# RWKV-7 elementwise tiles made in the projections instead of the scan, and projection weights split once per stream

## The chip, the cores and the metric

One Trainium2 chip, one core of it. The metric is the device time of one execution of the whole program in microseconds (us). The core has five engines that run side by side: TensorE (PE, matrix products; PEld are its weight loads), VectorE (DVE), ScalarE (ACT), GpSimd (POOL) and SyncE (SP), which here mainly issues DMA transfers. Each engine takes its instructions in the order in which the program holds them, and a waiting instruction holds up what stands behind it on its engine.

## The reference

A trunk of two layers (width 1024, 16 heads of 64 channels) for 1024 prompt tokens and for 8 short sequences of 8 sample tokens. Layer 0 mixes by a convolution, layer 1 by RWKV-7; each layer also has attention to a memory and an MLP of hidden width 4096. The change touches the RWKV-7 mixer alone:

```python
r = xr @ w_r;  k = xk @ w_k;  v = xv @ w_v            # projections of shifted, mixed inputs
decay = exp(-exp(w_log))                              # w_log from w0 + tanh(xw @ w1) @ w2
a = sigmoid(a0 + (xa @ a1) @ a2);  g = sigmoid(xg @ g1) @ g2
kk = k * k_k;  kk = kk / max(sqrt(sum(kk * kk)), L2_EPS)    # per head
k = k * (1 + (a - 1) * k_a)
y, s = wkv7_scan(r, decay, k, v, -kk, kk * a, s0)           # s: 64x64 per head, step by step
y = standardize(y) * lnx_g + lnx_b
bonus = sum(r * k * r_k) * v                                # per head
out = ((y + bonus) * g) @ w_o
```

## The kernel before

Channels lie on the 128 partitions in 8 blocks (a block is a *pair* of heads, index `m`), tokens run along the free axis. All wide products take float32 operands that are split into a high and a low half: `split` (L95) casts the high half on ScalarE (L96) and subtracts it for the low half on VectorE (L97), and `prod` (L138) does three matmuls (L142 to L144) for each product. Weights come from memory as tiles `raw` and become `wt` with both halves.

**Two streams.** Stream A is part 0 (512 prompt tokens, in column tiles of 256), stream B part 1 (the other 512 prompt tokens and the 64 sample tokens, in column tiles of 288). Each stream is a generator that runs conv, attention, MLP of layer 0, then the RWKV projections (`projections`, L729), the RWKV scan in chunks of 64 tokens (`scan`, L1088: A chunks 0 to 7, B the samples and chunks 8 to 15), the output projection (`mixer_out`, L893), attention and MLP of layer 1. B's scan needs A's last state. `pace` (L916) interleaves the two: each `yield` gives a cost, and the stream with the lower sum of costs goes next. A timeline scheduler then sets the order of each engine, which is fixed before the program runs. A_d and B_d are the PSUM accumulators of the two streams.

**Projections.** `project` (L866) does one of the three wide products, r, k and v in turn, block by block, and stores each result block (L847, issued by ScalarE) in the memory tile `scr[part][m]`, which has six rows: v, r, k, decay, a, g. Beside it run generators handed in as `sides`: `hidden` (L797) makes the hidden layers of the low-rank products, `lora` (L849) their outputs. The hidden layers of w and a share the tile `one`; so `lora("a")` runs last, when all else of the projections is done. A keeps the low halves of its 24 weight tiles: `load` (L106) with `share` puts them in the memory tiles `low` (`put`, L99), and B loads them from there rather than subtracting again.

**Scan.** `prep` (L1153) loads one chunk (`ld` four rows, `v` one row; eight DMAs each, one per pair, L1151, on SyncE's queue) and makes of it, in tiles of 128x512: kk, its square, the cumulative sum of the log decay (a VectorE scan), two exponentials, the products a, r, b and k with them (`ar`, `bk`), the sums of squares (`ss`, four matmuls on `sq`), and the bonus (`bon`, a product with `bones`, the matrix of ones per head). `invert`, `solve` and `step` are the recurrence itself. Its banks are p_pp, p_pz and p_half. `finish` (L1452) normalizes, applies lnx_g, lnx_b, bonus and gate on GpSimd, and stores `yg`. `prep` of one chunk, `inverse` of the chunk before and `rest` of the one before that run interleaved (`run`, L1514).

## Time and profile before

| | |
|---|---|
| time, median of 3 runs | 3836.46 us (3828.97 to 3836.49) |
| time of the profiled execution | 3837.42 us |
| span of the profiled execution | 3835.7 us |
| TensorE busy | 3623.9 us (94%) |
| VectorE busy | 2351.6 us (61%) |
| ScalarE busy | 1610.0 us (42%) |
| GpSimd busy | 660.7 us (17%) |
| mean granted clock of TensorE | 0.955 |
| moved by DMA | 456.03 MB, mean 119 GB/s |

The span is what the trace covers; the program's time is 1.7 us more. Busy TensorE time contains time at a reduced clock, so a busy share of 94% is not 94% of its peak. In the page's pictures a span is cut into 40 slices of 96 us.

The stretches that matter here, in us from the start: A's projections beside B's first MLP 1335 to 1747; A's scan 1747 to 2130 (beside it the end of B's MLP, B's norm and the start of B's projections); B's projections, A's memory layer, A's output projection and the start of its attention 2130 to 2460; B's scan to about 2850, beside A's attention and second MLP; then B's output projection, attention and MLP, with A's MLP until about 3395.

### The profile page before, as it was taken

The page shows a single profiled execution, that of the slowest core. Times are in us where ns is not written, and L with a number is a line of the kernel's source. Part 1 is how long each engine was busy: PE and PEld are TensorE (multiplying, and loading weights), DVE is VectorE, ACT ScalarE, POOL GpSimd, SP SyncE. Part 2 cuts the span into 40 slices and gives each one's busy share as a digit, 9 for nine tenths or more (in the row PEclk, how much of TensorE's full clock was granted, in tenths as well). Part 3 has the DMA queues.
Part 4 walks back from the last instruction along what each step waited for, and adds up shares of the span by engine and source line. Part 5 has one row for each costly group of instructions (what it writes and reads, how often), then busy time and mean ns, then how long its engine had stood idle before and what let it go on. Part 6 is the DMA issues. An engine that isn't in the chain of part 4 may idle for free.

```text
span 3835.7 us, 75763 instructions
## 1 busy us (share of the span) xinstructions
PE 3623.9 (94%) x30906; PEld 3369.6 (88%) x30906; DVE 2351.6 (61%) x4479; ACT 1610.0 (42%) x3190; POOL 660.7 (17%) x704
## 2 busy tenths in 40 slices
PE   8989979999999999999979998879999999989998
...
PEclk9999989999999999999979998889899999989998
...
GB/s 226 132 53 129 80 67 106 102 114 170 153 90 83 126 151 152 159 138 112 85 88 109 232 254 146 111 93 70 54 113 120 114 120 197 121 72 83 83 83 64
DMA packets 333004, 456.03 MB, mean 119 GB/s; under 512 B 155248, under 2 KB 247664, under 8 KB 332656
## 3 DMA queue, kind: packets, MB, share of 16 engines
...
q14 instruction: 105, 0.86, 0.1%
...
## 4 chain that ended last, share of the span: by engine, by line
PE 77%; DVE 11%; ACT 4%; DMA 4%; issue 2%; POOL 1%; SPq 1%; ACTq 0%; DVEq 0%; POOLq 0%
PE B_d L142 11%; PE B_d L144 11%; PE B_d L143 11%; PE A_d L142 10%; PE A_d L143 9%; PE A_d L144 9%; PE A_d L362 3%; PE B_d L362 2%; DMA scr<-t_st 1%; SPq L1151 1%; PE A_hd L810 1%; PE A_d L442 1%; PE B_sa L608 1%; DVE wt L97 1%; PE B_sa L610 1%
## 5 line engine op out<-in xcount | busy, mean ns | idle before, releaser
L97 DVE TENSOR_TENSOR wt<-raw,wt 128x1024 fp32r<-128x1024 f32 x447 | 567.3, 1272 | 476.9 <-ACT wt L96 473.0
L96 ACT CAST wt<-raw 128x1024 fp32r<-128x1024 f32 x488 | 508.5, 1047 | 502.2 <-PE B_d L144 268.6
L142 PE MATMUL B_d<-hAB,wt 128*128 128x288 f32 (+1 forms) x2240 | 673.6, 303 | 15.4 <-ACT hAB L96 6.3
L143 PE MATMUL B_d<-hBB,wt 128*128 128x288 f32 (+1 forms) x2240 | 668.5, 299 | 1.2 <-DVE hBB L97 1.1
L144 PE MATMUL B_d<-hAB,wt 128*128 128x288 f32 (+1 forms) x2240 | 666.2, 298 | 0.3 <-DVE wt L97 0.3
L142 PE MATMUL A_d<-hAA,wt 128*128 128x256 f32 x2240 | 639.1, 288 | 15.0 <-ACT hAA L96 13.6
L143 PE MATMUL A_d<-hBA,wt 128*128 128x256 f32 x2240 | 642.4, 288 | 3.4 <-DVE hBA L97 3.4
L144 PE MATMUL A_d<-hAA,wt 128*128 128x256 f32 x2240 | 632.8, 285 | 2.5 <-POOL wt L97 2.2
L142 PEld LDWEIGHTS A_d<-hAA,wt 128*128 128x128 f32 x2240 | 429.0, 192 | 25.1 <-ACT hAA L96 16.8
L142 PEld LDWEIGHTS B_d<-hAB,wt 128*128 128x128 f32 x2240 | 425.4, 191 | 24.5 <-ACT hAB L96 7.5
L143 PEld LDWEIGHTS A_d<-hBA,wt 128*128 128x128 f32 x2240 | 430.2, 192 | 14.3 <-DVE hBA L97 5.6
L144 PEld LDWEIGHTS A_d<-hAA,wt 128*128 128x128 f32 x2240 | 428.6, 192 | 7.3 <-POOL wt L97 2.6
L143 PEld LDWEIGHTS B_d<-hBB,wt 128*128 128x128 f32 x2240 | 427.2, 191 | 6.5 <-DVE hBB L97 3.7
L711 POOL TENSOR_TENSOR t_sg<-t_ev 128x256 f32<-128x256 f32 (+1 forms) x256 | 185.5, 725 | 1418.2 <-ACT t_ev L709 1329.3
L144 PEld LDWEIGHTS B_d<-hAB,wt 128*128 128x128 f32 x2240 | 426.1, 190 | 2.3 <-issue 0.7
L142 PE MATMUL B_d<-u,wt 128*128 128x288 f32 x1024 | 307.1, 301 | 0.0
L144 PE MATMUL B_d<-u,wt 128*128 128x288 f32 x1024 | 303.3, 299 | 0.0
L143 PE MATMUL B_d<-u,wt 128*128 128x288 f32 x1024 | 303.3, 298 | 0.0
L143 PE MATMUL A_d<-u,wt 128*128 128x256 f32 x1024 | 288.2, 282 | 0.0
L144 PE MATMUL A_d<-u,wt 128*128 128x256 f32 x1024 | 288.2, 282 | 0.0
L142 PE MATMUL A_d<-u,wt 128*128 128x256 f32 x1024 | 287.4, 282 | 0.0
L97 DVE TENSOR_TENSOR u<-t_sg,u 128x256 fp32r<-128x256 f32 (+1 forms) x256 | 130.4, 510 | 149.9 <-ACT u L96 149.6
...
## 6 DMA issues: line engine op xcount, KB each, us to landing
raw<-in_mlp_up_dram SPq DMA_DIRECT2D x128, 512.0 KB, 3.6
raw<-in_mlp_dn_dram SPq DMA_DIRECT2D x128, 512.0 KB, 3.6
raw<-in_rw_w_dram SPq DMA_DIRECT2D x64, 512.0 KB, 4.2
ld<-scr SPq DMA_DIRECT2D x136, 128.0 KB, 3.2
wf<-in_w_in_dram SPq DMA_DIRECT2D x32, 512.0 KB, 4.0
raw<-in_xa_w_q_dram SPq DMA_DIRECT2D x32, 512.0 KB, 3.6
raw<-in_xa_w_o_dram SPq DMA_DIRECT2D x32, 512.0 KB, 3.6
raw<-in_ck_dram SPq DMA_DIRECT2D x32, 512.0 KB, 3.6
```

The costliest lines, as they stand in the source:

```text
L96: self.nc.scalar.copy(hi, src)
L97: (engine or self.nc.vector).tensor_tensor(lo, src, hi.bitcast(F32), SUB)
L142: self.nc.tensor.matmul(out, lhsT=wh, rhs=mh, start=(i == 0), stop=False)
L143: self.nc.tensor.matmul(out, lhsT=wh, rhs=ml, start=False, stop=False)
L144: self.nc.tensor.matmul(out, lhsT=wl, rhs=mh, start=False, stop=(i == last))
L362: nc.tensor.matmul(ps[:, :n], lhsT=wt[:, 0, k * P:k * P + P], rhs=h[:, k, t0:t0 + n], start=(k == 0), stop=(k == NC8 - 1))
L442: nc.tensor.matmul(ps[hs], lhsT=dg[:, q, h], rhs=two[h][:, 2 * q:2 * q + 512], start=(q == 0), stop=(q == pairs - 1))
L608: nc.tensor.matmul(out[:, h2], lhsT=wt.rearrange("p i t -> p (i t)"), rhs=moving[:, 0], start=start, stop=stop)
L610: nc.tensor.matmul(out[:64, h2], lhsT=wt[:, 0], rhs=moving[:, 1], start=False, stop=False)
L711: nc.gpsimd.tensor_mul(sg[:, :n], r[:, :n], r[:, :n])
L810: nc.tensor.matmul(ps[:, :n], lhsT=w1[:, m:m + P], rhs=hc[:, :n], start=(c == 0), stop=(c == NC8 - 1))
L1151: nc.sync.dma_start(out=dst[..., m * 64:m * 64 + 64], in_=scr[part][m][:, slots, t0:t0 + 64])
```

## The change

In words:

- The elementwise part of `prep` goes into a new generator `stage(m, c0)` in `projections`, which works on one pair and some of its tokens: 256 columns in A (16 stages), 192 in B (24 stages). `staged` runs the stages one after another in a single tile `ld` of seven rows: load six rows of `scr`, compute in place, store seven rows in a new memory tile `tls[part][m]`. The rows of `tls` are kk·e, r·e, b·e, k·e (four operands of the recurrence), v, the gate with lnx_g, and bonus and lnx_b with the gate.
- The per-head sums of squares and the exponentials at the ends of chunks stay in two constant-pool tiles, `sums` and `ends`. The sums are now matmuls of one column on 64 rows; the bonus product is 256 or 192 columns wide instead of 512.
- `project` takes steps of `staged` during its last product, after all column tiles of a block; what is left runs at the end (`yield from tiles_of`). `hidden(4, "a")` moves beside the first product and `lora("a")` beside the last, with a tile `la` of its own in place of the shared `one`. The rows of `scr` are in a new order.
- `prep` loads `ar`, `bk` and `v` ready-made from `tls`, in a buffer `ld` that is now threefold. `finish` loads two rows instead of one and does three GpSimd operations instead of five.
- `low`, `share` and `put` are gone: B subtracts its own low halves.

```diff
-    def put(self):
-        if self.due:
-            dst, wt = self.due
-            self.nc.sync.dma_start(out=dst, in_=wt[:, 1].bitcast(F32))
-            self.due = None
-    def load(self, src, cols=1024, rows=P, lo=None, slot=None, share=None):
-        self.put()
...
-        if share is not None and self.part:
-            self.nc.scalar.copy(wt[:, 0], raw)
-            self.nc.sync.dma_start(out=wt[:, 1].bitcast(F32), in_=share)
-            return wt
...
-    low = [[dram.tile([P, 1024], F32, name=f"low{i}_{m}") for m in range(NC8)] for i in range(3)]
+    tls = [[dram.tile([P, 7, n], F32, name=f"tls{i}_{m}") for m in range(NC8)] for i, (_, n, _) in enumerate(PARTS)]
+    sums = [const.tile([P, NC8, n], F32, name=f"sums{i}") for i, n in enumerate((8, 9))]
+    ends = [const.tile([P, NC8, n], F32, name=f"ends{i}") for i, n in enumerate((8, 16))]
...
-        weights = s.weights([(a["rw_w"][i, m], 1024, P, None, None, low[i][m]) for i in range(3) for m in range(NC8)])
...
-        one, lh = (hp.tile([P, np_], F32R, name=f"l{n}") for n in "wh")
+        weights = s.weights([(a["rw_w"][i, m], 1024, P) for i in range(3) for m in range(NC8)])
+        lw, la, lh = (hp.tile([P, np_], F32R, name=f"l{n}") for n in "wah")
         lg = hp.tile([P, 2, np_], F32R, name="lg")
-        hid = {"w": one, "a": one, "h": lh}
...
+        half, pieces = (192, (0, 3, 6)) if part else (256, (0, 4))
+        ld = hp.tile([P, 7, half], F32, name="ld")
+        kk, t1, rst = (hp.tile([P, half], F32, name=n) for n in ("kk", "t1", "rst"))
...
+        def stage(m, c0):
+            nch = half // 64
+            tail_in = c0 + nch > 8
+            e_runs = cuts[1:] if tail_in else cuts[:1]
+            w, r, ag, k, v, g, bo = (ld[:, i] for i in range(7))
+            nc.scalar.activation(kk, k, AF.Copy, scale=col("k_k", m))
+            nc.scalar.activation(t1, k, AF.Square, scale=col("k_k", m))
+            ps = s.bank()
+            for i in range(nch):
+                for hs in (slice(0, 64), slice(64, P)):
+                    nc.tensor.matmul(ps[hs, i:i + 1], lhsT=t1[hs, 64 * i:64 * i + 64], rhs=bones[hs, hs][:, :1],
+                                     start=True, stop=True)
+            nc.vector.tensor_scalar_max(sums[part][:, m, c0:c0 + nch], ps[:, :nch], L2_MIN)
+            nc.vector.tensor_tensor_scan(out=w, data0=last_rst if tail_in else rst, data1=w, initial=0.0, op0=MUL, op1=ADD)
+            for e, l in zip(e_runs, runs(w, c0)):
+                nc.scalar.activation(e[:, :, 1:], l, AF.Exp, scale=-DECAY)
+            nc.scalar.activation(w, w, AF.Exp, scale=DECAY)
+            yield .3
+            nc.scalar.activation(t1, ag, AF.Identity, scale=col("k_a", m), bias=less[:, m:m + 1])
+            nc.vector.scalar_tensor_tensor(out=ag, in0=kk, scalar=-1.0, in1=ag, op0=MUL, op1=MUL)
+            nc.vector.scalar_tensor_tensor(out=t1, in0=t1, scalar=1.0, in1=k, op0=ADD, op1=MUL)
+            nc.vector.scalar_tensor_tensor(out=bo, in0=r, scalar=col("r_k", m), in1=t1, op0=MUL, op1=MUL)
+            nc.gpsimd.tensor_tensor(ag, ag, w, MUL)
+            nc.gpsimd.tensor_tensor(k, t1, w, MUL)
+            for i, (e, l, x1, x2, x3) in enumerate(zip(e_runs, (64, DSEQ), runs(r, c0), runs(kk, c0), runs(w, c0))):
+                e0, e1 = (8, 16) if i else (c0, min(8, c0 + nch))
+                nc.gpsimd.tensor_copy(ends[part][:, m, e0:e1], e[:, :, l])
+                nc.gpsimd.tensor_tensor(x1, x1, e[:, :, 1:], MUL)
+                nc.vector.tensor_tensor(x3, x2, e[:, :, :l], MUL)
+            yield .3
+            ps = s.bank()
+            nc.tensor.matmul(ps[:, :half], lhsT=bones, rhs=bo, start=True, stop=True)
+            nc.vector.tensor_tensor(bo, v, ps[:, :half], MUL)
+            nc.vector.scalar_tensor_tensor(out=bo, in0=bo, scalar=col("lnx_b", m), in1=g, op0=ADD, op1=MUL)
+            nc.scalar.activation(g, g, AF.Copy, scale=col("lnx_g", m))
+            yield .3
+        def staged():
+            old = None
+            for m in range(NC8):
+                yield 0
+                for c0 in pieces:
+                    if old is not None:
+                        nc.sync.dma_start(out=old, in_=ld)
+                    ts = slice(64 * c0, 64 * c0 + half)
+                    nc.sync.dma_start(out=ld[:, :6], in_=scr[part][m][:, :, ts])
+                    yield from stage(m, c0)
+                    old = tls[part][m][:, :, ts]
+            nc.sync.dma_start(out=old, in_=ld)
...
                         nc.scalar.copy(t[:, :n], ps[:, :n])
-                        store(t, m, (slot + 1) % 3, t0, n)
+                        store(t, m, (1, 3, 4)[slot], t0, n)
                         yield cost(n)
                         for side in sides:
                             yield next(side, 0)
+                    if slot == 2 and m0 and tt == tiles[-1]:
+                        for _ in range(1 + 3 * len(pieces)):
+                            yield next(tiles_of, 0)
                     if m0 == 6 and after is not None:
                         yield from mix(after, tt)
         for tt in tiles:
             yield from mix(0, tt)
-        yield from project(0, 2, hidden(1, "w", [AF.Tanh]))
-        yield from project(1, 3, hidden(5, "gh", [AF.Sigmoid, AF.Sigmoid]), lora("w", 3))
-        yield from project(2, None, hidden(4, "a", [AF.Copy]), lora("gh", 5))
-        s.put()
-        yield from lora("a", 4)
+        tiles_of = staged()
+        yield from project(0, 2, hidden(1, "w", [AF.Tanh]), hidden(4, "a", [AF.Copy]))
+        yield from project(1, 3, hidden(5, "gh", [AF.Sigmoid, AF.Sigmoid]), lora("w", 0))
+        yield from project(2, None, lora("a", 2), lora("gh", 5))
+        yield from tiles_of
...
-BUF = dict(w=5, bon=2, at=2, ar=2, Aq=2, UV=2, AV=2, BK=2, v=2, pcs=3)
+BUF = dict(w=5, ld=3, at=2, Aq=2, UV=2, AV=2, BK=2, v=2, pcs=3)
...
     def load(dst, c, slots):
         part, t0 = (1, 512) if c is None else (c // 8, c % 8 * 64)
         for m in range(NC8):
-            nc.sync.dma_start(out=dst[..., m * 64:m * 64 + 64], in_=scr[part][m][:, slots, t0:t0 + 64])
+            nc.sync.dma_start(out=dst[:, m], in_=tls[part][m][:, slots, t0:t0 + 64])
...
+        part, n = (1, 8) if sam else (chunk // 8, chunk % 8)
+        ld = new([P, 8, 4, 64], "ld")
+        load(ld, chunk, slice(0, 4))
+        ar, bk = ld[:, :, :2], ld[:, :, 2:]
         v = w512("v")
-        load(v, chunk, 0)
-        ar = new([P, 8, 2, 64], "ar")
-        bk = new([P, 8, 2, 64], "bk")
-        kk = w512()
-        nc.vector.tensor_tensor(v3(kk), v3(k), bvec("k_k"), MUL)
-        sq = w512()
-        nc.scalar.activation(sq, kk, AF.Square)
-        L = ws
-        nc.vector.tensor_tensor_scan(out=L, data0=masks["rst"], data1=ws, initial=0.0, op0=MUL, op1=ADD)
...
-        bp = ag
-        nc.vector.scalar_tensor_tensor(out=bp, in0=kk, scalar=-1.0, in1=ag, op0=MUL, op1=MUL)
-        nc.gpsimd.tensor_tensor(bk[:, :, 0], v3(bp), v3(En), MUL)
-        km = t1
-        nc.vector.scalar_tensor_tensor(out=km, in0=t1, scalar=1.0, in1=k, op0=ADD, op1=MUL)
-        nc.gpsimd.tensor_tensor(ar[:, :, 1], v3(r), v3(E) if sam else E[:, :, 1:], MUL)
-        nc.gpsimd.tensor_tensor(bk[:, :, 1], v3(km), v3(En), MUL)
-        rk = w512()
-        t = w512()
-        nc.gpsimd.tensor_tensor(v3(t), v3(r), bvec("r_k"), MUL)
-        nc.vector.tensor_tensor(rk, t, km, MUL)
...
-        ss = bank("pp")
-        for q in range(4):
-            nc.tensor.matmul(ss[:, 2 * q:2 * q + 2], lhsT=sq[:, q * P:q * P + P], rhs=bones[:, ::64], start=True, stop=True)
...
+        d4 = d32[:, :16].rearrange("p (c i) -> p c i", i=2)
+        nc.vector.tensor_copy(d4, sums[part][:, :, n].unsqueeze(2).broadcast_to([P, 8, 2]))
         yield
...
-        sb = bank("pp")
-        nc.tensor.matmul(sb, lhsT=bones, rhs=rk, start=True, stop=True)
-        bon = w512("bon")
-        nc.vector.tensor_tensor(bon, v, sb, MUL)
-        return dict(chunk=chunk, ar=ar, at=at, Aq=Aq, UV=UV, AV=AV, BK=BK, bon=bon, pcs=pcs)
+        return dict(chunk=chunk, ar=ar, at=at, Aq=Aq, UV=UV, AV=AV, BK=BK, pcs=pcs)
...
-        gg = w512("gg")
-        load(gg, chunk, 5)
+        gb = new([P, 8, 2, 64], "gb")
+        load(gb, chunk, slice(5, 7))
         nc.gpsimd.tensor_mul(y, y, rs)
-        nc.gpsimd.tensor_tensor(v3(y), v3(y), bvec("lnx_g"), MUL)
-        nc.gpsimd.tensor_tensor(v3(y), v3(y), bvec("lnx_b"), ADD)
-        nc.gpsimd.tensor_add(y, y, w["bon"])
-        nc.gpsimd.tensor_mul(y, y, gg)
+        nc.gpsimd.tensor_mul(v3(y), v3(y), gb[:, :, 0])
+        nc.gpsimd.tensor_add(v3(y), v3(y), gb[:, :, 1])
```

**Order, TensorE at the end of A's projections.** Before, A's first scan matmuls (L1208, the sums of squares into p_pp, and L1381, the state product into p_pz) stand among the matmuls of B's MLP (B_d from the hidden activations u):

```order
L142 MATMUL B_d_18243<-u_10533,wt_17998 128x288
L143 MATMUL B_d_18243<-u_10533,wt_17998 128x288
L1208 MATMUL p_pp_17544<-c_bones_17477,w_17525 128x2 x4
L144 MATMUL B_d_18243<-u_10533,wt_17998 128x288
L142 MATMUL B_d_18243<-u_10533,wt_17998 128x288
L143 MATMUL B_d_18207<-u_10533,wt_17998 128x288
L144 MATMUL B_d_18207<-u_10533,wt_17998 128x288
L143 MATMUL B_d_18243<-u_10533,wt_17998 128x288
L144 MATMUL B_d_18243<-u_10533,wt_17998 128x288
L1381 MATMUL p_pz_18343<-S_18341,ar_17521 64x64 x16
L142 MATMUL B_d_18269<-u_10533,wt_18149 128x288
L143 MATMUL B_d_18269<-u_10533,wt_18149 128x288
```

After, the last stages of A stand there (L895 the sums from the scaled square t1, L917 the bonus product from `ld`, both with the constant c_bones), then the scan's first matmuls (L1243, L1396), then the first matmul of B's projections (L126; hAB is the high half of B's mixed input):

```order
L895 MATMUL A_d_17930<-c_bones_12789,t1_12785 64x1 x8
L917 MATMUL A_d_17952<-ld_12783,c_bones_12789 128x256
L895 MATMUL A_d_17997<-c_bones_12789,t1_12785 64x1 x8
L917 MATMUL A_d_18019<-ld_12783,c_bones_12789 128x256
L895 MATMUL A_d_18028<-c_bones_12789,t1_12785 64x1 x8
L917 MATMUL A_d_18050<-ld_12783,c_bones_12789 128x256
L895 MATMUL A_d_18059<-c_bones_12789,t1_12785 64x1 x8
L917 MATMUL A_d_18081<-ld_12783,c_bones_12789 128x256
L1243 MATMUL p_pp_18177<-ld_18155 128x128
L1243 MATMUL p_pp_18178<-ld_18155 128x128
L1396 MATMUL p_pz_18921<-S_18919,ld_18155 64x64 x2
L126 MATMUL B_d_20540<-hAB_19945,wt_20289 128x288
```

Seven such pairs of L895 and L917 stand one behind another, and the last matmul of B's MLP is ahead of all seven; between the first of them stand only small matmuls of B's norm.

**Order, SyncE's queue at the same place.** Before, A's first scan loads (L1151) follow on the raw tiles of the low-rank weights (raw2) and of B's MLP weights (mlp_dn):

```order
L120 DMA raw_17996<-in_mlp_dn_dram 128x1024
L835 DMA raw2_17375<-in_a2_dram 64x128 x2
L835 DMA raw2_17407<-in_a2_dram 64x128 x2
L120 DMA raw_18147<-in_mlp_dn_dram 128x1024
L835 DMA raw2_17425<-in_a2_dram 64x128 x2
L120 DMA raw_18264<-in_mlp_dn_dram 128x1024
L120 DMA raw_18396<-in_mlp_dn_dram 128x1024
L1132 DMA rst_17501<-in_con_dram 128x512
L1151 DMA ld_17503<-scr0_0_73 128x4x64
L1151 DMA ld_17503<-scr0_1_74 128x4x64
```

After, stores from `ld` into `tls` (L931, L936) and loads of `ld` from `scr` (L933) alternate, with nothing between them, up to the first scan loads (L1215):

```order
L931 DMA tls0_5_94<-ld_12783 896x1x256
L933 DMA ld_12783<-scr0_6_79 128x6x256
L931 DMA tls0_6_95<-ld_12783 896x1x256
L933 DMA ld_12783<-scr0_6_79 128x6x256
L931 DMA tls0_6_95<-ld_12783 896x1x256
L933 DMA ld_12783<-scr0_7_80 128x6x256
L931 DMA tls0_7_96<-ld_12783 896x1x256
L933 DMA ld_12783<-scr0_7_80 128x6x256
L936 DMA tls0_7_96<-ld_12783 896x1x256
L1215 DMA ld_18155<-tls0_0_89 128x4x64
L1215 DMA ld_18155<-tls0_1_90 128x4x64
```

The loads of weight tiles that stood ahead of the scan have moved away from the last stages; the scan's loads come right behind the last store.

**Order, TensorE in B's projections.** Before, the end of B's projections (L856, `lora("a")`: the hidden layer lw with the weight w2) stands among A's norm (L251, L255) and A's wide matmuls (hAA and hBA are the high and low halves of A's activations):

```order
L251 MATMUL A_d_25773<-c_means_64,t_acc_25735 128x1 x2
L856 MATMUL B_d_25456<-lw_20156,w2_25451 128x288 x2
L856 MATMUL B_d_25462<-lw_20156,w2_25451 128x288 x2
L251 MATMUL A_d_25994<-c_means_64,t_acc_25928 128x1
L255 MATMUL A_d_25773<-c_ident_62,nv_25774 128x128 x2
L251 MATMUL A_d_25994<-c_means_64,t_acc_25928 128x1
L856 MATMUL B_d_25474<-lw_20156,w2_25469 128x288 x2
L142 MATMUL A_d_26080<-hAA_25728,wt_25732 128x256
L856 MATMUL B_d_25480<-lw_20156,w2_25469 128x288 x2
L143 MATMUL A_d_26080<-hBA_25729,wt_25732 128x256
```

After, B's stages stand among such work; here the third stage, with seven wide matmuls of A between its two groups of matmuls:

```order
L128 MATMUL A_d_25198<-hAA_25046,wt_25052 128x256
L895 MATMUL B_d_24661<-c_bones_20316,t1_20310 64x1 x6
L126 MATMUL A_d_25198<-hAA_25046,wt_25052 128x256
L127 MATMUL A_d_25198<-hBA_25047,wt_25052 128x256
L128 MATMUL A_d_25198<-hAA_25046,wt_25052 128x256
L126 MATMUL A_d_25198<-hAA_25046,wt_25052 128x256
L127 MATMUL A_d_25198<-hBA_25047,wt_25052 128x256
L128 MATMUL A_d_25198<-hAA_25046,wt_25052 128x256
L126 MATMUL A_d_25198<-hAA_25046,wt_25052 128x256
L917 MATMUL B_d_24702<-ld_20308,c_bones_20316 128x192
L126 MATMUL B_d_24712<-hAB_19945,wt_24408 128x288
```

What moved: the low-rank tail of B is gone from there, and a pair of small groups (L895, L917) for each of B's 24 stages has come among the wide matmuls of A and B.

## Rows read from the trace of the kernel before

**Rows 1.** Which slices TensorE (PE) fills and what clock it had, from the page: engine, tenths

```profile
PE 3623.9 (94%) x30906; PEld 3369.6 (88%) x30906; DVE 2351.6 (61%) x4479; ACT 1610.0 (42%) x3190; POOL 660.7 (17%) x704
...
PE   8989979999999999999979998879999999989998
...
PEclk9999989999999999999979998889899999989998
```

**Rows 2.** Busy time by stage: stretch, us, each engine, granted clock, DMA share, GB/s

```profile
1030.00:1335.00 305.00, 305.00 (x2441) 304.38 (x2440) 155.57 (x310) 101.16 (x183) 29.17 (x42) 1.00 0.31 98
1335.00:1747.00 412.00, 411.77 (x3170) 408.17 (x3170) 189.70 (x348) 198.33 (x434) 32.78 (x48) 1.00 0.48 150
1747.00:2130.00 383.00, 342.76 (x4609) 293.09 (x4608) 310.80 (x697) 209.04 (x422) 114.36 (x103) 0.89 0.36 98
2130.00:2460.00 330.00, 305.55 (x2281) 286.31 (x2280) 156.27 (x325) 166.47 (x352) 24.59 (x26) 0.95 0.65 200
2460.00:2850.00 390.00, 349.88 (x4759) 286.29 (x4759) 311.74 (x657) 184.59 (x373) 137.60 (x105) 0.87 0.27 73
```

**Rows 3.** TensorE's longest waits in 1747 to 2130: waiter, releaser, us in total, times, longest

```profile
PE p_pp L1235 <- issue: 5.2, 2, 3.4
PE p_pp L1245 <- DVE Aq L1229: 5.1, 3, 2.2
PE p_half L1342 <- DVE T L1337: 5.1, 2, 2.7
PE B_d L255 <- DVE nv L236: 3.7, 1, 3.7
```

**Rows 4.** Groups by line, VectorE: shapes xcount | busy us, mean ns | idle before, releaser

```profile
L1171 DVE TENSOR_TENSOR_SCAN ld<-rst,ld 128x512 f32<-128x512 f32 x17 | 26.8, 1578 | 2.2 <-DMA v<-scr 2.2
...
L1212 DVE TENSOR_SCALAR d<-p_pp 64x8 f32<-64x8 f32 x68 | 11.1, 163 | 3.8 <-PE p_pp L1208 3.0
```

**Rows 5.** Busy time of one stretch of A's scan

```profile
1915.00:1980.00 65.00, 47.95 (x664) 36.66 (x662) 55.36 (x126) 33.65 (x68) 27.56 (x29) 0.68 0.40 107
```

**Rows 6.** DMA issues: out<-in, queue, xcount, KB each, median us to landing

```profile
raw<-in_mlp_up_dram SPq DMA_DIRECT2D x128, 512.0 KB, 3.6
...
ld<-scr SPq DMA_DIRECT2D x136, 128.0 KB, 3.2
...
low<-wt SPq DMA_DIRECT2D x24, 512.0 KB, 3.0
...
xa<-xA SPq DMA_DIRECT2D x4, 1024.0 KB, 5.1
...
xA<-xa SPq DMA_DIRECT2D x4, 1024.0 KB, 6.1
...
raw<-in_mem_dram SPq DMA_DIRECT2D x4, 512.0 KB, 8.6
```

**Rows 7.** Groups by line: ScalarE, VectorE and GpSimd operations of 256 columns

```profile
L269 ACT ACTIVATE t_sq<-xA 128x256 f32<-128x256 f32 x98 | 39.4, 415 | 69.7 <-DVE xA L305 27.5 <-DVE xA L725 20.7 <-DVE xA L513 13.0
...
L782 ACT ACTIVATE t_dl<-xA,rest 128x256 f32<-128x256 f32 x48 | 23.2, 506 | 2.9 <-DVE hBA L97 2.5
...
L783 DVE SCALAR_TENSOR_TENSOR hc<-xA,vec,hc 128x256 f32<-128x256 f32 x48 | 23.1, 484 | 25.2 <-ACT hc L782 25.2
...
L711 POOL TENSOR_TENSOR t_sg<-t_ev 128x256 f32<-128x256 f32 (+1 forms) x256 | 185.5, 725 | 1418.2 <-ACT t_ev L709 1329.3 <-DVE nv L252 77.6 <-DVE u L97 5.2
```

**Rows 8.** Groups by line, TensorE: small and fp32 matmuls

```profile
L1381 PE MATMUL p_pz<-S,ar 64*64 64x64 f32 x512 | 25.9, 247 | 1.6 <-ACT rs L1463 1.6
...
L1256 PE MATMUL p_pp<-w,c_bones 128*128 128x512 f32 x34 | 22.8, 757 | 1.4 <-ACT BK L1246 1.4
...
L1208 PE MATMUL p_pp<-c_bones,w 128*128 128x2 f32 x136 | 21.2, 274 | 1.8 <-ACT AV L1253 1.8
```

**Rows 9.** Timeline: eight issues of the scan's load, start us, us

```profile
1754.16 5.06 SPq L1151 DMA_DIRECT2D ld<-scr  x8
```

**Rows 10.** Groups by line, VectorE: the low half of a weight tile

```profile
L97 DVE TENSOR_TENSOR wt<-raw,wt 128x1024 fp32r<-128x1024 f32 x447 | 567.3, 1272 | 476.9 <-ACT wt L96 473.0 <-DMA raw<-in_g_dram 1.3 <-DMA wt<-low 1.1
```

79 lines of the change are left out of this document (31 added, 48 removed).

## The prediction, as put on record

> **What bounds the kernel now.** I read the page first: TensorE's matrix row is busy 94% of the span, and in the picture of 40 slices it stands at 9 wherever the clock row does [rows 1]. So time is lost only where TensorE waits or has its clock halved. The busy time by stage shows where that is [rows 2]. In the stretch from 1335 to 1747 us (A's projections beside B's MLP) TensorE is busy 411.77 of 412 us at full clock: what is added to TensorE there is paid, what is added elsewhere is hidden. Three stretches lose something. I call *loss* the span minus busy time times granted clock: A's scan, 383 − 342.76 × 0.89 = 78 us; B's late projections and A's output and attention, 330 − 305.55 × 0.95 = 40 us; B's scan, 390 − 349.88 × 0.87 = 86 us. That is 204 us in all, the most that the change can win. In A's scan VectorE is busy 310.80 of 383 us, and the longest of TensorE's waits there end on VectorE [rows 2, 3]. TensorE alone carries the rest: 2441 wide matmuls in 305 us, 0.125 us each.
>
> **What leaves the scans.** Eight elementwise groups of VectorE go out of each of the 17 chunks: 26.8 + 17.4 + 15.6 + 15.3 + 13.6 + 12.5 + 11.5 + 11.1 = 123.8 us, 7.3 us a chunk [rows 4] (the first and the last of the eight). One small copy comes in. ScalarE and GpSimd lose work too, but neither is full there (209 and 114 us of 383 [rows 2]). In A's scan 8 × 7.3 = 58 of 311 us of VectorE go, and the scan now stands beside B's projections throughout, 10 to 15 us of wide matmuls per chunk, where before two chunks had 3 to 4 us. The worst piece of before, 65 us at a clock of 0.68 (a loss of 32 us [rows 5]), was A's scan with nothing of B's but a norm. I take half of the loss of A's scan back: −40 us, bounds 0 and −78 (all of it). In B's scan the same relief meets a loss: the order now puts chunks 8 to 15 there without one wide matmul between them, where before 32 to 196 of A's stood in each. Without cover the scan's own chain sets the pace. I set gain against loss: 0, bounds −50 (relief alone) and +45 (eight chunks 5 to 6 us longer).
>
> **What one stage costs.** This is the term that decides. A stage works in a single buffer `ld`: load six rows, compute, store seven, and only when the store has landed may the next load start. Nothing of a stage overlaps with the next. For A: the load is 768 KB. Loads of 512 KB take 3.6 us from issue to landing, of 1024 KB 6.1 (`xA<-xa`, the same 1 KB pieces) [rows 6], so 4.9. The store is 896 KB between `low<-wt` (512 KB, 3.0) and `xa<-xA` (1024 KB, 5.1) [rows 6]: 4.6. Between them lies a chain of five ScalarE operations of 256 columns at about 0.45 us (0.415 and 0.506 [rows 7]), two VectorE ones at 0.48 [rows 7], half of a 128x512 fp32 matmul (0.757 [rows 8]), two more VectorE ones, and hops: 2.2 + 1.0 + 0.4 + 1.0 + 0.6 = 5.2 us. A stage of A takes 14.7 us. GpSimd's four operations at about 0.7 [rows 7] end beside it. B's stages (192 columns: loads of 576, stores of 672 KB) come to 13 us. Bounds: 10 (512 KB prices at both ends, 3.5 us of chain), and 18 to 20 (contended transfers: 8.6 us for 512 KB in `raw<-in_mem` [rows 6]).
>
> The Trainium skill, page "DMA: Bandwidth & Descriptors", section "Anatomy of one DMA", fits 2.0 us plus the bytes at 436 GB/s, measured on GpSimd's queue. As an estimate by it, the two transfers take 3.8 and 4.1 us, a stage of A 13.1, and seven of them 92 us where I have 103; but it gives 4.4 us for the 1024 KB that took 5.1 and 6.1 here [rows 6], so the rows are kept. The page "Trainium Kernel Development and Optimization", section "Best Practices", asks for double buffers so that transfers overlap with work; this change has one buffer. No run here shows two. Estimated from the terms above, a stage would then be paced by its 5.2 us of compute, seven would take 36 us, and the total would be 67 us lower.
>
> **The hole after A's projections.** Nine of A's 16 stages stand among B's MLP matmuls, 16 us or more of them from stage to stage: covered, 0 (up to +18 if stages take 2 us more). But then B's MLP has run out, and the order has the last seven stages one behind the other on TensorE, with only the small matmuls of B's norm among the first. B's projections stand behind A's first scan matmuls, which need all eight `tls` tiles. TensorE therefore waits 7 × 14.7 = 103 us, less 3.5 us of wide matmuls after the ninth stage, plus the end: two VectorE operations (1.0), the store (4.6), eight loads issued in 5.06 us and 3.2 us to landing [rows 6, 9]. 103 − 3.5 + 13.9 = 113, less 3 us of norm matmuls: **+110 us**, bounds 77 and 147 (stages of 10 and of 20 us). SyncE waits in the same chain, so no weights are loaded beside it. Before, A's scan began among B's MLP matmuls, without a hole.
>
> **B's stages.** Their 24 stand among A's output projection and attention. From a stage's last matmul to the next one's, 14 steps hold 13 us or more of wide matmuls (covered), nine hold 2 to 9 us, 54 us together (some 430 matmuls at 0.125 [rows 2]). Nine times 13 is 117, so TensorE idles 63 us. Waits cost the clock too: in A's scan 40 us of idle time went with 38 of clock loss [rows 2]. I add half of 63: 32. Of the 40 us lost there before, the end of B's `lora` goes and the rest is counted in the gaps. 63 + 32 − 40 = **+55 us**, bounds +14 (stage of 10 us) and +173 (stage of 18, where the other 14 steps wait too).
>
> **The small terms.** The `bones` product of 512 columns per chunk becomes 16 of 256 and 24 of 192, the same 8704 columns: 0. The 68 matmuls for the sums become 272 of one column on half the rows. At 0.156 us (21.2/136 [rows 8]) that is +32; at the price of other 64-row matmuls (0.05, 25.9/512 [rows 8]) +3. Being 64-row ones, I take +6. The 24 `low` stores and loads of 512 KB go; 24 VectorE subtractions at 1.27 us [rows 10] and 24 weights more to split come in for B, hidden under VectorE's 156 of 330 us [rows 2]; if that cover went it would be 30 us. `lora` for `a` moves forward, ACT table loads rise by 34: ScalarE is busy 198 of 412 us there, 0.
>
> **Sum.** +110 + 55 − 40 + 0 + 6 = +131 us on the profiled execution's 3837.4, which stands 1 us over the median of the runs: **3968 us**, 3.4% slower.
>
> **Rivals.** *Relief wins (faster).* The scans lose their VectorE limit at both places, and stages are short. At 10 us a stage the hole is 78 and B's gaps +14, with +3 for small matmuls 95; the scans give back 78 and 50. That is −33: 3804 us. It needs more than 95 of the 128 us that I allow the scans, and a stage at its floor; for it speaks VectorE's 81% in A's scan, against it that TensorE's waits there come to 40 us in all. Chance 0.06. *Stages contend (much slower).* In the projections the DMA engines are already 48% and 65% busy [rows 2], and each stage brings 1.3 to 1.7 MB. At 18 us, hole 133, B's gaps +173, A's nine covered stages +18, scans −20, matmuls +20: +324, 4161 us. Against it: in the hole the transfers run alone. Chance 0.17. *They cancel.* Stages of 10 us and scans that win 98 (78 + 14 + 6): within 0.2%, chance 0.03. The change could fail to do what it says only if the order above did not hold on the chip; the engines take their instructions in order, so I give this nothing of its own.
>
> **How the numbers follow.** My forecast has 0.74. A measurement of this kernel tells 0.2% from no change. Slower by more is forecast and contention, 0.91; the same 0.03; faster 0.06. The range leaves out the relief rival, the upper part of contention and some of the forecast's low side (stage of 11 us, scans winning 70): 3880 to 4130.
>
> **What would show it.** In the changed profile: one stretch of some 110 us with TensorE nearly idle at the end of A's projections, SyncE waiting there in turn on stage results and landings; stage to stage 14 to 15 us; B's stages 13 us apart with idle TensorE where A's norm and softmax stand; VectorE per chunk 7 us lower; chunks 8 to 15 close together, with no wide matmul. Wrong would be: stages under 11 us, a hole under 70 us, or a loss in the two scans under 40 us together.

## The result

The changed kernel takes 4156.15 us (median of 4 runs, 4150.76 to 4158.6), the kernel before 3836.47: a ratio of 1.0833, interval 1.0812 to 1.0854. The forecast was 3968 us, range 3880 to 4130: the direction was right, the size was not, and the time lies above the range.

The page of the changed kernel, the same lines as [rows 1]: TensorE's busy share falls from 94 to 90%, and the pictures of busy time and of clock have new holes about slice 19 and between 23 and 34.

```profile
PE 3742.8 (90%) x31360; PEld 3456.2 (83%) x31360; DVE 2366.0 (57%) x4661; ACT 1721.0 (41%) x3421; POOL 581.5 (14%) x747
...
PE   8989979999999999971899878689989799999998
...
PEclk9989989999999999985899989789865899999999
```

Its busy time by stage, to be read beside [rows 2] (stretch, length, then busy time and instruction count of TensorE, weight loads, VectorE, ScalarE, GpSimd; the last three columns are granted clock, DMA share and GB/s). The stretches are cut where this kernel's stages lie: A's projections and nine stages; the hole; A's scan; B's projections; B's 24 stages; B's scan; what follows.

```profile
0.00:1335.00 1335.00, 1260.14 (x8663) 1146.63 (x8664) 897.93 (x1596) 502.51 (x992) 200.90 (x238) 0.97 0.37 116
1335.00:1840.00 505.00, 495.38 (x3849) 487.36 (x3848) 254.95 (x475) 251.79 (x528) 66.70 (x91) 1.00 0.44 137
1840.00:1970.00 130.00, 22.14 (x157) 15.39 (x155) 47.58 (x120) 27.65 (x60) 20.37 (x40) 0.51 0.37 125
1970.00:2325.00 355.00, 332.11 (x4384) 276.95 (x4384) 242.08 (x607) 220.47 (x463) 27.44 (x23) 0.88 0.40 102
2325.00:2400.00 75.00, 63.25 (x422) 59.38 (x424) 30.48 (x33) 39.39 (x67) 4.18 (x4) 0.89 0.77 239
2400.00:2870.00 470.00, 380.85 (x2831) 357.85 (x2832) 240.56 (x534) 210.38 (x454) 79.32 (x142) 0.85 0.48 151
2870.00:3240.00 370.00, 324.65 (x4383) 255.48 (x4381) 205.87 (x507) 144.99 (x287) 46.36 (x42) 0.72 0.32 79
3240.00:3600.00 360.00, 342.59 (x2761) 339.25 (x2762) 193.63 (x310) 156.51 (x271) 84.41 (x91) 0.97 0.46 146
3600.00:4149.00 549.00, 521.70 (x3922) 517.87 (x3919) 252.89 (x488) 167.33 (x304) 51.77 (x77) 0.97 0.27 84
```

With loss as the prediction defines it, span minus busy time times granted clock, most of the difference can be placed. The stretch from 1840 to 1970 loses 130 − 22.14 × 0.51 = 119 us. The whole trace of before, cut in the same way, loses 365 us, and this one 676: 310 of the 313 us by which the span grew. So what grew is mainly time in which TensorE stands still or runs at half its clock.

| stretch | loss before, us | loss after, us | change | predicted |
|---|---|---|---|---|
| up to A's last stages | 114 | 122 | +8 | 0 |
| hole at A's last seven stages | 0 | 119 | +119 | +110 |
| A's scan | 78 | 63 | −15 | −40 |
| B's projections and stages | 31 | 165 | +134 | +55 |
| B's scan | 93 | 136 | +43 | 0 |
| after B's scan | 50 | 71 | +21 | 0 |
| not placed (TensorE's own work is in it) | | | +3 | +6 |

B's projections and scan of before are cut here where the scan's first and last matmul stand, and not at 2460 as in [rows 2]; their rows, in the same columns:

```profile
2130.00:2397.00 267.00, 245.97 (x1686) 229.77 (x1685) 112.93 (x245) 136.10 (x294) 11.39 (x15) 0.96 0.68 214
2397.00:2850.00 453.00, 409.46 (x5354) 342.84 (x5353) 355.08 (x738) 214.95 (x432) 150.79 (x116) 0.88 0.31 82
```

These losses are coarse, since the mean clock of a stretch is taken for all busy time in it. Over the whole trace in one piece, the same formula gives 3835.7 − 3623.9 × 0.955 = 375 us before and 4149.0 − 3742.8 × 0.915 = 724 us after, 349 apart instead of 310. So the last row of the table cannot tell how much TensorE's own work grew. The stages' matmuls themselves show it (line, engine, operation, shapes, count of records, then busy us and mean ns, then idle time before):

```profile
L917 PE MATMUL B_d<-ld,c_bones 128*128 128x192 f32 x48 | 15.0, 400 | 6.0 <-DVE ld L907 6.0
L895 PE MATMUL B_d<-c_bones,t 64*64 64x1 f32 x288 | 14.9, 215 | 29.6 <-ACT t L891 26.3 <-ACT t_st L849 3.3
...
L917 PE MATMUL A_d<-ld,c_bones 128*128 128x256 f32 x32 | 14.2, 534 | 17.9 <-DVE ld L907 17.9
L895 PE MATMUL A_d<-c_bones,t 64*64 64x1 f32 x256 | 12.8, 217 | 83.0 <-ACT t L891 82.9
```

The sums (L895) take 27.7 us, where they took 21.2 before, and the bonus products (L917) 29.2 instead of 22.8 [rows 8]: some 13 us more together, part of it at the lower clock.

**One stage, in the hole.** The chain of work that ended last, between 1840 and 1970, followed in order of time (start, duration, what; some short steps are left out):

```profile
1900.14 4.30 DMA tls<-ld
1904.52 4.89 DMA ld<-scr
1910.45 1.04 PE A_d L895 x16
1911.51 0.61 ACT t L904
...
1913.45 0.92 POOL ld L909
...
1916.16 0.52 ACT ld L921
1916.73 4.31 DMA tls<-ld
```

From store to store are 16.6 us. The store takes 4.3 and the load 4.9, close to what was estimated (4.6 and 4.9). The compute between the landing and the next store takes 7.3 us, where the prediction had 5.2. It had counted five ScalarE operations, four of VectorE and the bonus product in a row, with GpSimd beside them. The trace has the square, the sums (1.04 us at half clock), the scaling (which must wait for the sums, since it overwrites their operand t1), a chain through VectorE, GpSimd (0.92 us) and VectorE again, and three more operations. The sums and GpSimd's product were not in the prediction's list.

**One stage of B.** ScalarE's instructions in one of B's stages, in order of time (start us, us, engine, line, operation, and in brackets what ended its idle time before):

```profile
2711.40 0.46 ACT L890 ACTIVATE kk<-ld,vec 128x192 f32<-128x192 f32 x1 [3.60 <-DMA ld<-scr]
2711.76 0.44 ACT L891 ACTIVATE t<-ld,vec 128x192 f32<-128x192 f32 x1
2712.11 0.35 ACT L901 ACTIVATE ones<-ld 128x192 f32<-128x192 f32 x1
2712.49 0.36 ACT L902 ACTIVATE ld<-ld 128x192 f32<-128x192 f32 x1
2712.76 1.03 ACT L95 CAST wt<-raw 128x1024 fp32r<-128x1024 f32 x1
2713.70 0.41 ACT L257 ACTIVATE t_acc<-xA 128x256 f32<-128x256 f32 x1
2714.01 0.41 ACT L257 ACTIVATE t_sq<-xA 128x256 f32<-128x256 f32 x1
2714.32 0.53 ACT L904 ACTIVATE t<-ld,less,vec 128x192 f32<-128x192 f32 x1
2715.95 1.05 ACT L95 CAST wt<-raw 128x1024 fp32r<-128x1024 f32 x1 [1.09 <-PE A_d L128]
2719.74 0.46 ACT L921 ACTIVATE ld<-ld,vec 128x192 f32<-128x192 f32 x1 [2.74 <-DVE ld L920]
```

L890, L891, L901, L902, L904 and L921 are the stage's; the two L95 (casts of A's weights) and the two L257 (A's norm) are A's. The stage's six operations take 2.6 us, and from the first to the end of the last pass 8.8 us, since A's work on ScalarE, VectorE and TensorE stands among them. Over B's 24 stages the median of this time is 9.3 us. B's last eleven stages follow each other every 17.5 to 21.5 us, most of them at 18, not every 13.

ScalarE's table loads stand in this chain too, and the prediction put them at nothing. It foresaw 34 more of them; the traces have 56 before and 90 after, 1.28 us each. Two lines have nearly all that came in, the stage's first exponential (L901) and `lora` (L849, L862 in the kernel before, where it had three):

```profile
L849 ACT ACT_TABLE_LOAD x22 | 28.2, 1283 | 1.5 <-ACT t_st L949 1.2
...
L901 ACT ACT_TABLE_LOAD x14 | 18.0, 1283 | 1.0 <-DVE nt L223 0.8
```

Seven of the 14 at L901 stand in B's stages, inside the chain of a stage. No run isolates what they cost.

The other direction is seen in the waits (waiter, releaser, us in total, times, longest) of ScalarE, VectorE and TensorE between 2400 and 2870:

```profile
ACT kk L890 <- DMA ld<-scr: 77.1, 22, 5.9
...
DVE ld L899 <- DMA ld<-scr: 72.1, 23, 10.3
...
DVE sums L897 <- PE B_d L895: 14.9, 10, 8.7
...
PE B_d L895 <- ACT t L891: 26.3, 13, 7.3
PE A_d L546 <- DVE e L539: 14.6, 6, 4.5
```

ScalarE stands 77 us at the first instruction of a stage (L890), waiting for the stage's load, and VectorE 72 us at its own (L899). What is queued behind is A's: casts, norms, exponentials. So TensorE waits both at the stages' matmuls (L895) and at A's (L546, the transposes of A's softmax). The stages in turn wait for TensorE: VectorE stands 14.9 us at L897 for the sums, whose matmuls stand behind A's in TensorE's order.

### The profile page after: what moved, and what is told of

Same layout as the page of the kernel before. It is cut to its first block, busy times and chain, and to the rows that moved or that the text cites. A ratio compares the mean times of both kernels' runs of the same rounds, so it can differ in the third digit from the quotient of the medians.

```text
span 4149.0 us, 77156 instructions
## 1 busy us (share of the span) xinstructions
PE 3742.8 (90%) x31360; PEld 3456.2 (83%) x31360; DVE 2366.0 (57%) x4661; ACT 1721.0 (41%) x3421; POOL 581.5 (14%) x747
## 4 chain that ended last, share of the span: by engine, by line
PE 68%; DMA 11%; DVE 9%; ACT 8%; issue 2%; POOL 1%; SPq 1%; ACTq 0%; DVEq 0%; POOLq 0%
PE B_d L126 9%; PE B_d L128 9%; PE B_d L127 9%; PE A_d L126 8%; PE A_d L127 8%; PE A_d L128 7%; DMA ld<-scr 4%; DMA tls<-ld 4%; PE A_d L350 3%; PE B_d L350 2%; PE p_pp L1243 2%; DVE wt L96 1%; ACT wt L95 1%; PE B_hd L797 1%; PE A_hd L797 1%
## 5 line engine op out<-in xcount | busy, mean ns | idle before, releaser
L96 DVE TENSOR_TENSOR wt<-raw,wt 128x1024 fp32r<-128x1024 f32 x471 | 590.8, 1256 | 478.8 <-ACT wt L95 474.0
L95 ACT CAST wt<-raw 128x1024 fp32r<-128x1024 f32 x512 | 533.6, 1046 | 521.9 <-PE B_d L128 232.3
L126 PE MATMUL B_d<-hAB,wt 128*128 128x288 f32 (+1 forms) x2240 | 678.3, 305 | 35.9 <-ACT hAB L95 25.7
L126 PE MATMUL A_d<-hAA,wt 128*128 128x256 f32 x2240 | 641.5, 289 | 31.8 <-ACT hAA L95 19.2
L126 PEld LDWEIGHTS B_d<-hAB,wt 128*128 128x128 f32 x2240 | 428.4, 192 | 46.6 <-ACT hAB L95 29.7
L126 PEld LDWEIGHTS A_d<-hAA,wt 128*128 128x128 f32 x2240 | 431.1, 193 | 42.7 <-ACT hAA L95 23.1
L126 PE MATMUL B_d<-u,wt 128*128 128x288 f32 x1024 | 303.2, 298 | 2.3 <-ACT u L95 1.9
L126 PE MATMUL A_d<-u,wt 128*128 128x256 f32 x1024 | 287.5, 282 | 0.0
```

The costliest lines, as they stand in the source:

```text
L95: self.nc.scalar.copy(hi, src)
L96: (engine or self.nc.vector).tensor_tensor(lo, src, hi.bitcast(F32), SUB)
L126: self.nc.tensor.matmul(out, lhsT=wh, rhs=mh, start=(i == 0), stop=False)
```

## The experiments

Twelve kernels, each timed in rounds beside the kernel before. Names L... are lines of the changed kernel.

### What the parts cost: no_stages, no_compute, no_matmuls, split_only

**split_only** is the kernel before with only `low` taken out, so that `share` and `put` have nothing to do:

```diff
-        weights = s.weights([(a["rw_w"][i, m], 1024, P, None, None, low[i][m]) for i in range(3) for m in range(NC8)])
+        weights = s.weights([(a["rw_w"][i, m], 1024, P, None, None, None) for i in range(3) for m in range(NC8)])
```

> The kernel before with only the second part of the change: B splits its own projection weights, the low halves are neither stored nor loaded. Theory (hidden under VectorE's slack): within 8 us of 3836. Rival (VectorE's 24 subtractions of 1.27 us come on the path): about 30 us slower, 3866.

Measured: 3853.2 us, ratio 1.0038, interval 1.0025 to 1.0051: 17 us slower, between the two. The second part of the change is not free, as the prediction had it. The loss grew in the two scans; here is A's:

```profile
1745.00:2140.00 395.00, 346.40 (x4617) 296.98 (x4617) 323.67 (x709) 210.22 (x425) 109.61 (x102) 0.88 0.31 83
```

It loses 395 − 346.40 × 0.88 = 90 us instead of 78, with VectorE 13 us busier, as B's projections begin beside it. B's scan loses 110 instead of 93, though VectorE is as busy there as before (355 us), so these 17 us come with the new order. B's late projections lose 25 instead of 31.

**no_stages** drops `staged` and `stage` and stores each result straight into its row of tls:

```diff
-            nc.scalar.dma_start(out=scr[part][m][:, slot, t0:t0 + n], in_=t[:, :n])
+            nc.scalar.dma_start(out=tls[part][m][:, slot, t0:t0 + n], in_=t[:, :n])
...
-        yield from tiles_of
```

> The changed kernel with all stages left out: the projections store their results straight into tls (one row twice), sums and ends are constants. The lighter scan, its loads and the own splitting of B remain. It shows what the scans give back when the stages cost nothing. Theory of the prediction: A's scan gives back 40 us and B's 50, splitting costs 16: about 3836 + 16 - 90 = 3762. Rival (the scans are bound by their own chain of small steps, not by VectorE's share): they give back 20 us or less in all, 3830 or more.

Measured: 3793.5 us, ratio 0.9899, interval 0.988 to 0.9919. Against split_only that is 60 us for the lighter scans. Its stretches of A's scan, B's projections and B's scan:

```profile
1714.00:2075.00 361.00, 343.68 (x4521) 291.91 (x4520) 239.34 (x581) 183.52 (x372) 42.27 (x50) 0.89 0.35 92
2075.00:2348.00 273.00, 258.83 (x1790) 245.58 (x1790) 127.21 (x251) 145.40 (x313) 7.11 (x10) 0.97 0.60 188
2348.00:2752.00 404.00, 373.26 (x4979) 306.94 (x4978) 267.86 (x653) 195.27 (x400) 50.99 (x40) 0.88 0.36 98
```

The losses are 361 − 343.68 × 0.89 = 55, 22 and 76 us, against 78, 31 and 93 before: A's scan gives back 23, B's projections and scan 26. Against split_only, which has the same splitting, A's scan gives back 35 and B's 34. Neither theory hit: the gain is some two thirds of the 90 us that the prediction's reasons would allow. VectorE is busy 239 us in A's scan instead of 311, and yet 55 us stay lost. That the chain of small steps keeps them is the likely reason, but is not shown.

**no_compute** keeps the stages' loads and stores on SyncE's queue and leaves out all that is computed between:

```diff
         def stage(m, c0):
-            nc.scalar.activation(kk, k, AF.Copy, scale=col("k_k", m))
...
+            yield .3
+            yield .3
             yield .3
```

> The changed kernel whose stages only load and store (what they compute is left out, sums, ends and the seventh row are constants); SyncE's queue and the transfers are as in the changed kernel. Theory (what costs in B's stages is that ScalarE, VectorE and TensorE wait in order for a stage's load, with A's own operations queued behind): the loss from 2325 us to the start of B's scan falls from 165 us to about 50, B's 24 stages take about 230 us instead of 468, a hole of about 60 us is left at A's last stages (seven of 9.4 us); no_stages' 3793 + 60 + 30 = about 3885. Rival (the transfers and SyncE's waits hold up weight loads): the loss before B's scan stays above 110, 3960 or more.

Measured: 3882.2 us, ratio 1.0125, interval 1.0111 to 1.0138, as the theory had it to 3 us. The stretch of B's stages:

```profile
2240.00:2500.00 260.00, 207.84 (x1387) 194.12 (x1387) 87.93 (x179) 89.27 (x193) 5.80 (x10) 0.86 0.81 248
```

It loses 260 − 207.84 × 0.86 = 81 us, where the changed kernel lost 165 before B's scan (no_stages loses 22 there). From 2325 on, as the expectation counts, it is 59, near its 50; but here seven of B's 24 stages have begun by then. The loads of B's 24 stages are issued within 239 us, some 8 to 12 us apart at the end, and ScalarE waits for none of them. One expected detail was wrong: there is no hole of 60 us, since A's stages, 11 us each without computing, are through at 1771, while B's MLP still runs. The transfers alone cost 3882.2 − 3793.5 = 89 us, the computing between them 274 us.

**no_matmuls** leaves out the two kinds of matmul in a stage (272 one-column ones, not the 320 that the expectation names, and 40 bonus products):

```diff
-                    nc.tensor.matmul(ps[hs, i:i + 1], lhsT=t1[hs, 64 * i:64 * i + 64], rhs=bones[hs, hs][:, :1],
-                                     start=True, stop=True)
-            nc.vector.tensor_scalar_max(sums[part][:, m, c0:c0 + nch], ps[:, :nch], L2_MIN)
+            nc.vector.tensor_scalar_max(sums[part][:, m, c0:c0 + nch], t1[:, :nch], 500.0)
...
-            nc.tensor.matmul(ps[:, :half], lhsT=bones, rhs=bo, start=True, stop=True)
-            nc.vector.tensor_tensor(bo, v, ps[:, :half], MUL)
+            nc.vector.tensor_tensor(bo, v, bo, MUL)
```

> The changed kernel with the matmuls of the stages left out, 320 groups of sums and 40 bonus products (the sums are replaced by a VectorE maximum with a constant, the bonus by a plain product), so that TensorE waits for no stage and has less to do; loads, stores and the rest of the stages stay. Theory (in B's stages TensorE loses time by waiting in order at the stages' small matmuls): the loss between 2325 and 2870 falls from 151 us to about 60, with 20 to 27 us less work and cover left for B's scan; about 3990. Rival (that loss is A's norm and softmax that lost their cover, and the stages' waits only hide it): 20 to 30 us for the work and little else, 4125.

Measured: 4019.3 us, ratio 1.0487, interval 1.0463 to 1.0511: 137 us below the changed kernel, nearer to the theory, but not for its reason. The loss before B's scan hardly falls: 174 us (44 from 2260 to 2400 and 130 in the next 305 us), where 60 were expected. The waits of TensorE and of ScalarE there:

```profile
PE A_d L546 <- DVE e L539: 32.0, 7, 7.6
...
ACT kk L890 <- DMA ld<-scr: 65.2, 17, 7.3
```

TensorE now waits for A's softmax, 32 us instead of 15, and ScalarE still stands 65 us before stages' loads. Taking TensorE out of the stages moves its wait to the next engine in order. What is won is won elsewhere. The stages get shorter, since they no longer wait for matmuls that stand behind wide ones: in B the median from the first ScalarE operation to the last is 7.0 us instead of 9.3. So A's stages are through at about 1909 instead of 1970 and the hole loses 49 us instead of 119; B's are through at 2705 instead of 2870, and the new order leaves wide matmuls beside B's scan (loss 61 us instead of 136). The matmuls left out are also 57 us of TensorE's busy time.

These runs make a ladder: 3836 (before) + 17 (splitting) − 60 (lighter scans) + 89 (transfers of the stages) + 137 (their computing on ScalarE, VectorE and GpSimd) + 137 (their matmuls) = 4156. The steps depend on their order, since each kernel has an order of instructions of its own.

### Which stream pays: a_only, b_stages

**a_only** has stages and lighter scan in A, and B's projections and scan of before:

```diff
-            yield from projections(s, ph, s.part, pair(s))
+            yield from (projections_old if s.part == 1 else projections)(s, ph, s.part, pair(s))
```

> Stages, tls and the lighter scan in stream A alone; B has the projections and the scan of the kernel before. Both split their own weights. B's projection tiles are smaller again; in the order B's projections now stand among A's last seven stages (4 to 18 us of wide matmuls each), and none is left beside A's scan. Theory (wide work is one stock: what covers A's stages is missing in A's scan): the hole is gone (116 us to under 20), the loss of A's scan rises from 63 to 130 or more, B's part is as before the change; about 3836 + 16 (splitting) + 10 + 70 = 3930. Rival (the hole is due to the stages' own length whatever stands beside them): the hole stays at 100 or more, 3960 or more, with A's scan at 63.

Measured: 3956.6 us, ratio 1.0319, interval 1.0292 to 1.0347. Its stretches of A's last stages and A's scan:

```profile
1840.00:2029.00 189.00, 152.31 (x934) 132.18 (x934) 121.24 (x293) 113.02 (x242) 25.02 (x39) 0.87 0.55 174
2029.00:2314.00 285.00, 244.14 (x3719) 201.48 (x3717) 169.85 (x440) 141.53 (x296) 26.86 (x22) 0.73 0.31 76
```

The first loses 189 − 152.31 × 0.87 = 56 us where the hole lost 119, the second 107 where A's scan lost 63; B's scan, in its old form, loses 127. The rival's hole is not there; the theory's direction holds, with less contrast than it had (under 20, and 130). The time is 27 us above the theory's 3930, near the rival's 3960; B's scan, which the theory left as it was, loses 17 us more than in split_only.

**b_stages** is the complement: stages in B alone, A's results stored straight into tls (as in no_stages, for part 0).

> The changed kernel with A's stages left out (A's projections store straight into tls, A's sums and ends are constants); B's 24 stages are complete. Theory (the stages of the two streams cost independently of each other): A's stages and hole are worth 957 - 853 = 104 us (a_only less split_only) and some 23 us that A's scan gives back, so 4156 - 127 = about 4030. Rival (the cost of B's stages comes from cover that A's stages have used up): B's stages alone cost 100 us or less over no_stages' 3793, 3895 or less.

Measured: 3967.5 us, ratio 1.0349, interval 1.0334 to 1.0364, between the two: B's stages alone cost 174 us over no_stages, and A's another 189 on top, where the theory had 127. The stretches of B's stages and of B's scan:

```profile
2240.00:2720.00 480.00, 391.85 (x2974) 372.59 (x2975) 249.96 (x552) 215.03 (x463) 80.75 (x148) 0.86 0.47 147
2720.00:3070.00 350.00, 292.92 (x4324) 232.35 (x4323) 201.46 (x493) 142.74 (x285) 47.55 (x42) 0.78 0.32 79
```

They lose 143 and 122 us, as in the changed kernel (146 and 136). So B's part of the error has nothing to do with A's hole.

### What cover is worth: cover_scan, cover_both, late_pool

Cover is wide work of one stream that TensorE can do while the other stream waits.

**cover_scan** changes one number of the planner:

```diff
-            yield .3
+            yield 2.0
```

(in three places)

> The changed kernel with one planner number altered: each of the three yields of a stage charges 2.0 instead of 0.3 to its stream. All instructions stay; in the order, chunks 9 to 13 of B's scan now have 9 to 13 us of A's wide matmuls each, where the changed kernel has none. Theory (B's scan is slow because no wide work stands beside it): the loss of B's scan falls from 154 us to about 90, as before the change, and the time from 4156 to about 4090. Rival (the scan itself became slower, for instance by its loads from tls): the loss stays at 150 and the time within 15 us of 4156.

Measured: 4152.0 us, ratio 1.0816, interval 1.08 to 1.0832. B's scan:

```profile
2862.00:3262.00 400.00, 379.37 (x5240) 320.79 (x5239) 247.63 (x579) 178.33 (x346) 60.17 (x62) 0.92 0.38 97
```

It loses 51 us instead of 136, a larger fall than the theory's, so the scan itself did not become slower. But the time is the rival's, 4 us below the changed kernel: by their rows B's stages lose 14 us more, the stretch before them 13, the end 21. The wide matmuls that cover one place are missing in another. (The loss of the whole trace falls by 28 us, its span by 7. The difference can't be placed; the loss counts all busy time at a lower clock as stretched by it, which need not hold for the scan's small matmuls.)

**cover_both** also sets `B_COST[1]` from 1.0 to 1.3.

> As cover_scan, and the cost factor of B's first MLP in the planner goes from 1.0 to 1.3, so that more of that MLP is left beside A's stages: three of A's stages stand without wide matmuls instead of seven. Theory (an uncovered stage of A costs its 16.5 us, a covered one nothing): the hole shrinks by 4 x 16.5 = 66 us against cover_scan, 4156 - 65 - 66 = about 4025. Rival (stages contend with the weight loads of the MLP and slow it): no more than 20 us below cover_scan.

Measured: 4092.8 us, ratio 1.0661, interval 1.0645 to 1.0677; 59 us below cover_scan, near the theory's 66 (the time itself, 4025, was missed by what cover_scan had missed). The hole loses 64 us instead of 121 in cover_scan, which is nearly all that was won: a stage of A that has cover costs next to nothing, as the prediction took it.

**late_pool** asks what holds B's projections back during the hole. B's norm is done at 1865 in the changed kernel, yet GpSimd's first instruction of B's projections (L742) starts at 1964.22, right behind A's last stage:

```profile
1963.60 0.67 POOL L913 TENSOR_TENSOR ld<-ld,ones 128x256 f32<-128x256 f32 x1
1964.22 0.39 POOL L742 COPY sh<-xB 128x8 f32<-128x8 f32 x1
```

and B's first projection matmul at 1972.8. The edit allocates the tiles of the stages when a stream's first stage begins, instead of with its other projection tiles:

```diff
+        def tiles_late():
+            hq = s.pool(ctx, "pq")
-        ld = hp.tile([P, 7, half], F32, name="ld")
+            ld = hq.tile([P, 7, half], F32, name="ld")
...
-        tiles_of = staged()
+        tiles_of = tiles_late()
```

> The changed kernel with one difference: the tiles of the stages (ld, kk, t1, rst, ones and the like, some 10 KB of each partition) are allocated when a stream's first stage begins, and not with its other projection tiles. In the order B's projections now stand among A's last seven stages (4 to 18 us of wide matmuls each, where there was none), none is left beside A's chunks 1 to 7, and B's stages and scan stand as in the changed kernel. So it is memory that held B's projections until A's stages were through. Theory (wide work is one stock, as in a_only): the hole's loss falls from 119 us to about 55, that of A's scan rises from 63 to about 105; 4156 - 25 = about 4130. Rival (the hole is a loss of its own, and closing it is clear gain): 4156 - 70 = 4085 or less.

Measured: 4114.5 us, ratio 1.0723, interval 1.0699 to 1.0747, 42 us below the changed kernel: between theory and rival. B's first projection matmul starts at 1868.9. The hole and A's scan:

```profile
1840.00:1974.00 134.00, 107.11 (x653) 92.97 (x651) 93.99 (x236) 81.19 (x181) 18.09 (x31) 0.85 0.53 172
1974.00:2280.00 306.00, 253.64 (x3642) 210.81 (x3644) 190.47 (x489) 155.94 (x324) 28.81 (x29) 0.75 0.36 93
```

They lose 43 and 116 us, 159 together, where the changed kernel lost 119 + 63 = 182. So the hole came from where the stages' tiles are allocated: with them among B's projection tiles, B's projections could start only when A's stages were through. That they lay on memory of A's projection tiles is inferred; no view shows addresses. And again most of what closes the hole is missing in A's scan.

### Shorter stages, and a smaller version: two_buffers, two_buffers_cover, inline

**two_buffers** halves the stages and gives them two buffers:

```diff
-        half, pieces = (192, (0, 3, 6)) if part else (256, (0, 4))
-        ld = hp.tile([P, 7, half], F32, name="ld")
+        half, pieces = 128, (0, 2, 4, 6, 8)[:5 if part else 4]
...
+                ld = hp.tile([P, 7, half], F32, tag="ld", name="ld", bufs=2)
...
+                nxt = fetch(k + 1) if k + 1 < len(todo) else None
+                yield from stage(ld, m, c0)
```

> The changed kernel with stages of 128 columns (32 in A, 40 in B, the last of each pair of B 64 sample columns) and two buffers ld, the load of the next stage issued ahead of the store of this one. Same arithmetic. Theory (stages are slow because load, compute and store stand in series): stages follow each other every 6 to 7 us instead of 16.5 for twice the columns, the hole of twelve short stages is 75 to 85 us instead of 120, B's 40 stages take 250 to 280 us instead of 468, and three of nine chunks of B's scan get cover; about 4020 us in all. Rival (stages are bound by their compute chain and the fixed cost of each instruction): 10 us or more per short stage, no gain, 4150 or more.

Measured: 4114.9 us, ratio 1.0720, interval 1.0702 to 1.0738: 41 us won of the 136 expected. ScalarE's wait for loads in B's stages:

```profile
ACT kk L890 <- DMA ld<-scr: 61.7, 23, 7.6
```

A's uncovered short stages come in pairs of 13.5 us (some 5 and 8.5), where one stage of twice the columns took 16.5, and B's 40 take 411 us instead of the 461 of 24, from the first bonus product to the last. The loss in B's stages is 145 us as before (146), and ScalarE still waits 62 us: with two buffers a load must still wait for the store before last, and there are nearly twice as many operations. The Trainium skill, page "Trainium Kernel Development and Optimization", section "Best Practices", asks for double buffers to let transfers overlap with work. The prediction's estimate for two buffers was 67 us; this run, which also halves the stages, gives 41.

**two_buffers_cover** adds `B_COST[1] = 1.1`.

> two_buffers with the planner's cost factor of B's first MLP at 1.1 instead of 1.0. In the order ten short stages of A instead of twelve stand without wide matmuls, and chunks 8 to 14 of B's scan have 10 to 14 us each. Theory (cover decides): the loss of B's scan falls from 89 to about 40 and the hole by 10 us; 4115 - 50 - 10 = about 4055. Rival (cover is one stock, what the scan gets is missing at the end, where B runs alone): less than 25 us below two_buffers, 4090 or more.

Measured: 4111.2 us, ratio 1.0726, interval 1.071 to 1.0742: the rival. B's scan loses 53 us instead of 85, and the total stays.

**inline** is an attempt to have some relief without stages, in the kernel before:

```diff
+                    if slot == 3 and part == 0:
+                        nc.vector.tensor_tensor_scan(out=t, data0=rst, data1=t, initial=0.0, op0=MUL, op1=ADD)
                     store(t, m, slot, t0, n)
+                    if slot == 4:
+                        t2 = s.small("st")
+                        nc.scalar.activation(t2[:, :n], t[:, :n], AF.Identity, scale=col("k_a", m), bias=less[:, m:m + 1])
+                        store(t2, m, 5, t0, n)
```

> The kernel before (with the shared low halves) and two of the elementwise steps moved without any stage: the cumulative sum of A's log decay is made on the tile of lora('w') just before it is stored, and (a - 1) * k_a is made by one ScalarE operation more on the tile of lora('a') and stored as a seventh row of scr. The scan of A loses two VectorE operations of a chunk, that of B one. Theory (the relief is worth what no_stages showed, in proportion: A's scan gave back 23 us for 7.3 us of VectorE a chunk): 2.4 of 7.3 us a chunk in A and 0.9 in B, some 10 us faster, 3826. Rival (so little is lost in the noise of a new order): within 5 us of 3836.

Measured: 3846.1 us, ratio 1.0036, interval 1.0023 to 1.0049: 10 us slower, which is neither the theory nor the rival. B's scan:

```profile
2413.00:2860.00 447.00, 383.86 (x5147) 317.40 (x5146) 341.45 (x726) 206.26 (x418) 147.20 (x117) 0.85 0.33 84
```

A's scan loses 372 − 334.31 × 0.91 = 68 us instead of 78, the 10 us expected; but B's scan, which had only lost an operation, loses 121 instead of 93. The likely reason is the other order that the scheduler made around it. No version that was tried beats the kernel before with its result complete.

## Why the prediction was wrong, point by point

The traces differ by 313 us, the forecast had 131. Of the 182 us between them, B's projections and stages have 79, B's scan 43, A's scan 25, the end 21.

- **The bound was read rightly.** By the table, TensorE's idle time and clock carry 310 of 313 us.
- **The small matmuls: right by luck.** +6 was taken for the sums, and they grew by 6.5 us. But the price per matmul was read wrongly: the 136 records of [rows 8] are 68 matmuls, two records each, as the 544 of L895 are 272. At the two prices named, with two records each, the growth would have been +64 and +6, not +32 and +3. The bonus products, put at 0 for equal columns, grew by 6.4 us.
- **The hole: right.** +110 predicted, 119 lost. After the first, its stages follow each other every 16.5 us instead of 14.7. Its reason was only half told: the order had no wide matmuls there, and the prediction took that as given. late_pool shows that it followed from where the tiles of B's stages are allocated.
- **B's stages: the step that failed.** "A stage of B 13 us" was mis-sized: 18 us and more. The transfers were right (4.6 and 4.5 us for load and store); the compute chain was taken at 5.2 us for a stage of A, and measures 7.3 us there and 8.8 us in the stage of B shown. With 13 us, 14 steps counted as covered and cost 0. Counted in the trace from bonus product to bonus product, these 14 hold 1952 wide matmuls, 230 us at the 0.118 us between their starts, and take 292 us. The nine others hold 42 us of wide matmuls and take 169, where the prediction had 54 and 117. The prediction's own upper end for this term, a stage of 18 where the other 14 steps wait too, was +173; measured are +134.
- **What was missing there altogether** is the other direction: it asked only what TensorE waits for at the stages' matmuls. ScalarE and VectorE wait for the loads, 77 and 72 us, with A's work queued behind, and the stages wait for TensorE. no_matmuls shows that without any matmul in the stages the loss before B's scan is still 174 us, no_compute that without the computing it is 81.
- **A's scan: right in direction, too large for this kernel.** −40 predicted, −15 here; no_stages has −23, or −35 against split_only, so the relief itself was nearly right. VectorE's 81% was a weak sign: the instructions that TensorE waited for in [rows 3] (L1229, L1337, L236) are not among the eight groups that left, and the longest entry there is no wait for VectorE.
- **B's scan: wrong.** "Relief 50 against 45" gave 0; the loss grew by 43. The missing cover, chunks 8 to 15 without a wide matmul, was seen, and priced at 5 to 6 us a chunk. In cover_scan the scan's loss is 85 us less with that cover, some 10 us a chunk. The relief was 17 us (no_stages), 34 against split_only, not 50.
- **The splitting: wrong.** Hidden, 0, was predicted; split_only has +17. The cover was read from the stretch 2130 to 2460, where VectorE is half free; but B's projections also run beside A's scan, where it is busy 81% [rows 2], and there the loss grew by 12 us.
- **The end: not foreseen.** +21 us after B's scan.
- **The rival of contention** gave 4161 us, 5 from the result, and its stage of 18 us. That is luck: the stages' transfers did not slow down (medians of 4.5 to 4.9 us), their computing did, and of its terms the scans (−20, measured +28) have the wrong sign. What the transfers cost without computing is the 89 us of no_compute.

What stays open: how much of the +21 at the end and of split_only's +17 is the cost of the edit and how much the other order of instructions that comes with every edit. inline moved B's scan by 28 us without touching more than one of its operations. What the 34 table loads cost is not tested; they are part of the 274 us of computing (no_compute has 54 of them in all, no_matmuls 96). And the split of the 274 us of computing between TensorE and the other engines depends on which is taken out first.
